# Seven-product gate/up stage: first-half token tiles turned and summed under the last two cross-attention outputs, second-half blocks loaded in place

## The chip, the cores and the metric

One core of one Trainium2 chip. The metric is the device time of one execution in microseconds (us): for the kernel before 2898.38, the median of 3 runs (2897.5 to 2900.68).

## What is computed

One decoder layer on x (2048 tokens of width D = 1024, float32): a token mixer, a cross-attention to 256 memory tokens, and a gated channel mixer of width 2816. The change touches the end of the second and the beginning of the third:

```python
...
    x = x + rmsnorm(xo @ w_xo, g_x_post)

    hf = rmsnorm(x, g_ffn_pre)
    ff = (jax.nn.silu(hf @ w_gate) * (hf @ w_up)) @ w_down
    x = x + rmsnorm(ff, g_ffn_post)
```

rmsnorm(x, g) is x * rsqrt(mean(x*x) + eps) * g, token by token.

## The kernel before, in words

TensorE's instructions stand in the order of the program. A scheduler orders the other engines' (VectorE, ScalarE, GpSimd, and SP, which issues the DMAs), and buffers come from pools that rotate. Tokens come in tiles of 128, so x is 16 tiles, 0 to 15. Precision: each float32 operand is split into a high part, a ScalarE cast to fp32r (L142), and a low part, a VectorE subtraction (L143); a product is hi·hi + hi·lo + lo·hi, three times the matmuls.

**Cross-attention outputs.** `c_out(t)` (L1091 on) makes the output of token tile t in 48 matmuls 128x512 (L1095), 24 for each half of the columns, then squares and sums it (ScalarE), scales it by gain and adds x (VectorE), takes the next norm's factor `rx2`, and stores the tile.

**Seven products.** gate and up use Strassen's scheme with seven products in place of eight. The tokens come in two halves of 8 tiles (first half tiles 0 to 7, second half 8 to 15). Even and odd token tiles on one side, the two halves of K = 1024 on the other, make 2 x 2 blocks; from these come seven operand blocks: B11 and B21 of the even tiles, B22 of the odd ones, and T1 = odd0 - even0, T2 = odd1 - T1, T3 = odd1 - odd0, T4 = T2 - even1, where 0 and 1 are the halves of K. Each block holds [128, 2 (hi, lo), 4, 512] numbers. The 22 column tiles of w_gate and of w_up come in 11 column pairs. `weights()` (L1246) loads a pair's weights (buffers `wr`), forms the weight sums on GpSimd (L1257 to L1263) and splits them into `w`, from a ring of ten buffers (`w4t`). `product` (L1273) makes 12 matmuls 128x512; a block takes 12 for gate and 12 for up, a pair 7 x 24 = 168. The order of the blocks in a pair is B11, T2, B21, T3, T1, T4, B22, into four PSUM tiles; sums of products on VectorE and the SwiGLU (L1280, L1281) follow, and `g` is stored.

**Tiles of the first half.** `d_load` (L1123) loads a tile `xtD` and multiplies it by `rx2` and the gain in one VectorE operation (L126); `d_transposed` turns it with 8 TensorE transposes (L1133) into PSUM. `d_even` (L1144) splits the turned tile into B11 and B21 and keeps a copy `hf`; `d_odd` (L1153) forms T1, T2, T3 (VectorE) and T4 (GpSimd, L1169) and splits them and B22. The loaded tiles rotate through the pool `tk` of three buffers, which also holds the last cross-attention tiles. The even tiles 0, 2, 4, 6 are turned under the outputs of tiles 14 and 15; the odd tiles 1, 3, 5, 7 inside the first pair, after its first products.

**Tiles of the second half** are turned one at a time between the first-half pairs 0 to 8 (`d_even_kept`, `d_odd_kept`, L1176 to L1199). Their blocks are kept as float32 in DRAM (`hc_d`); GpSimd makes the differences (L1192 to L1195). The even tile's copy `hf` has a pool of its own (`fh`); the odd tile's copy `ho` and its differences `t12` come from the ring of ten weight buffers.

**Half switch.** Behind the last pair of the first half the seven blocks are loaded back (L1354 to L1357), each in two halves of 512 KB through one buffer `hst`, and split again. The 11 pairs of the second half follow, and then the down product, whose weights `wd` are split by L142 and L143 as well (L1366 on).

Of the kernel before, what the change touches and what calls it, by code (L numbers as in the profile page):

```python
# [10 lines left out]
F32 = mybir.dt.float32  # L11
F32R = mybir.dt.float32r
# [37 lines left out]
def layer(ctx, tc, a, out):  # L50
# [1093 lines left out]
    def d_even(hc, t):  # L1144

        pt = d_transposed(t)
        for i, n in enumerate(("B11", "B21")):
            put(hc, n, t % 8 // 2, pt[:, i * 512:(i + 1) * 512])
        hf = ev.tile([P, T], F32, name="hf", tag="ev")
        sc.copy(hf, pt)  # L1150
        return hf

    def d_odd(hc, t, hf):  # L1153

        j = t % 8 // 2
# [12 lines left out]
        t4 = h12[:, 512:]
        gp.tensor_tensor(t4, t2, hf[:, 512:], ALU.subtract)  # L1169
        put(hc, "T4", j, t4)  # L1170
        put(hc, "B22", j, pt[:, 512:])

    def keep(name, j, src):
        sp.dma_start(hc_d[name][:, :, j * P:(j + 1) * P], q4(src))

    def d_even_kept(t):  # L1176
        pt = d_transposed(t)
        hf = fh.tile([P, T], F32, name="hf", tag="hf")
        sc.copy(hf, pt)
        for i, n in enumerate(("B11", "B21")):  # L1180
            keep(n, t % 8 // 2, hf[:, i * 512:(i + 1) * 512])
        return hf

    def d_odd_kept(t, hf):
        j = t % 8 // 2
        pt = d_transposed(t)
# [12 lines left out]
        keep("T3", j, hf[:, 0:512])  # L1199
# [9 lines left out]
    for t in range(NT):  # L1209
# [9 lines left out]
        if t == NT - 2:  # L1219
            esM.close()  # L1220
            esD = ExitStack()
            hpa = pool(esD, "hpa")
            ev = pool(esD, "ev", 4)
            gf = gain("g_ffn_pre")
            hc = {n: hpa.tile([P, 2, 4, 512], F32R, name="h" + n) for n in ("B11", "B21")}
            d_load(0)
            d_load(2)
            hfs = {}
# [56 lines left out]

    def pair(hv, n, hc, mids=()):
        mids = dict(mids)
        gens = [weights(w_, n) for w_ in (wg, wu)]
        pts, s = {}, {}

        def both(h, name, start, stop):
            if start:
                pts[name] = ps.tile([P, T], F32, name="pgu", tag="mm")
            for i in range(2):
                w = next(gens[i])
                product(pts[name], i, w, hc[h], start, stop)
                if (h, i) in mids:
                    mids[h, i]()
# [5 lines left out]
        both("B11", "X", True, False)
        s["1"] = ev.tile([P, T], F32, name="s1", tag="ev")
        sc.copy(s["1"], pts["X"])
        both("T2", "Y", True, False)
        s["16"] = ev.tile([P, T], F32, name="s16", tag="ev")
        v.tensor_tensor(s["16"], pts["Y"], s["1"], ALU.add)
        both("B21", "X", False, True)  # L1310
        sg = half.tile([P, 512], F32, name="sg", tag="half")
        swiglu(*lo_hi(pts["X"]), hv, 0, f, sg)
        both("T3", "Y", False, True)
        v.tensor_tensor(s["1"], pts["Y"], s["1"], ALU.add)
        both("T1", "Z", True, False)
# [3 lines left out]
        both("T4", "W", True, True)  # L1319
# [3 lines left out]
        both("B22", "Z", False, True)  # L1323
# [28 lines left out]
    for n in HC:  # L1352
        hc[n] = (hpa if n in ("B11", "B21") else hpb).tile([P, 2, 4, 512], F32R, name="h" + n)
# [117 lines left out]
```

## Time and profile before

| | |
|---|---|
| median of 3 runs | 2898.38 us (2897.5 to 2900.68) |
| the profiled execution's own time | 2900.78 us |
| its span on the core | 2899.0 us |
| mean granted TensorE clock | 0.981 of full speed |
| busy share of the span | TensorE 95%, VectorE 52%, ScalarE 38%, GpSimd 16% |
| DMA, mean over the span | 111 GB/s |

The span is what the profiler saw of the core from its first to its last instruction; the execution's own time is 1.78 us longer. Busy shares are means over stages with different limits, so a stage is read from its own waits and its own timeline. PE is TensorE, DVE VectorE, ACT ScalarE, POOL GpSimd, SP (in rows SPq) the engine that issues the DMAs; L1273 is line 1273 of the kernel. Names in rows have no buffer numbers: `pgu` is the PSUM tile of gate and up, `pt` a turned tile, `pxo` an output of the cross-attention, `hB` and `hT` the operand blocks, `w` a split weight.

### The profile page before, as it was taken

The page shows a single profiled execution, that of the slowest core. Times are in us where ns is not written, and L with a number is a line of the kernel's source. Part 1 is how long each engine was busy: PE and PEld are TensorE (multiplying, and loading weights), DVE is VectorE, ACT ScalarE, POOL GpSimd, SP SyncE. Part 2 cuts the span into 40 slices and gives each one's busy share as a digit, 9 for nine tenths or more (in the row PEclk, how much of TensorE's full clock was granted, in tenths as well). Part 3 has the DMA queues.
Part 4 walks back from the last instruction along what each step waited for, and adds up shares of the span by engine and source line. Part 5 has one row for each costly group of instructions (what it writes and reads, how often), then busy time and mean ns, then how long its engine had stood idle before and what let it go on. Part 6 is the DMA issues. An engine that isn't in the chain of part 4 may idle for free.

```text
span 2899.0 us, 35143 instructions
## 1 busy us (share of the span) xinstructions
PE 2767.6 (95%) x13420; PEld 2293.9 (79%) x13420; DVE 1510.5 (52%) x2393; ACT 1087.7 (38%) x2294; POOL 464.1 (16%) x337
## 2 busy tenths in 40 slices
PE   9989989999989999999979999997999999999998
PEld 6778768888877888888858777786888887888887
DVE  4363367787886555333475555555454543122244
ACT  4232137677776444222252333233333333120122
POOL 0000012212240000000013433331333210000022
PEclk9999989999999999999989999998999999999999
DMA  5443563534442543111133343334222234131153
GB/s 185 131 168 106 171 199 112 152 105 135 132 147 68 173 166 116 44 44 44 59 109 98 120 124 108 103 113 130 77 80 88 84 95 134 48 105 51 37 171 119
DMA packets 239713, 322.82 MB, mean 111 GB/s; under 512 B 14776, under 2 KB 183864, under 8 KB 239544
## 3 DMA queue, kind: packets, MB, share of 16 engines
q1 hardware_dynamic: 239224, 319.52, 34.7%
q8 instruction: 106, 1.74, 0.3%
q0 software_dynamic: 320, 1.05, 0.1%
q14 instruction: 63, 0.52, 0.1%
HBM read 224.96 MB, written 95.55 MB: 111 GB/s over the span
## 4 chain that ended last, share of the span: by engine, by line
PE 78%; DVE 8%; DMA 4%; ACT 3%; issue 1%; POOL 1%; SPq 0%; DVEq 0%; ACTq 0%; POOLq 0%
PE pgu L1273 26%; PE pdn L1385 16%; PE pxo L1095 6%; PE psc L1056 6%; PE pmix L870 5%; PE S L731 3%; PE o L792 3%; PE pu L287 2%; DVE p L773 2%; DVE nmx L738 2%; PE pv L303 2%; PE T L783 1%; PE pqk L287 1%; PE o L537 1%; PE S L870 1%
## 5 line engine op out<-in xcount | busy, mean ns | idle before, releaser
L1273 PE MATMUL pgu<-hT,w 128*128 128x512 f32 x2112 | 495.3, 394 | 27.6 <-ACT hT L142 21.0
L1273 PEld LDWEIGHTS pgu<-hT,w 128*128 128x128 f32 x2112 | 400.9, 190 | 115.8 <-ACT hT L142 22.3
L1385 PE MATMUL pdn<-wd,g 128*128 128x512 f32 x2112 | 481.7, 390 | 4.2 <-DVE wd L143 3.5
L1385 PEld LDWEIGHTS pdn<-wd,g 128*128 128x128 f32 x2112 | 397.3, 188 | 88.4 <-DVE wd L143 4.7
L1273 PE MATMUL pgu<-hB,w 128*128 128x512 f32 x1584 | 375.0, 394 | 16.5 <-ACT w L142 10.0
L143 DVE TENSOR_TENSOR w<-wr,w 128x512 fp32r<-128x512 f32 (+3 forms) x382 | 260.3, 707 | 214.7 <-ACT w L142 213.8
L1273 PEld LDWEIGHTS pgu<-hB,w 128*128 128x128 f32 x1584 | 299.5, 190 | 82.2 <-ACT w L142 11.2
L142 ACT CAST w<-wr 128x512 fp32r<-128x512 f32 (+3 forms) x384 | 202.0, 557 | 343.7 <-PE pgu L1273 206.4
L731 PE MATMUL S<-kt,q 128*128 128x512 f32 (+2 forms) x640 | 181.5, 399 | 34.6 <-ACT p L747 33.5
L747 ACT ACTIVATE p<-S,nmx 128x1024 f32<-128x1024 f32 (+3 forms) x192 | 167.4, 873 | 95.5 <-DVE nmx L740 44.1
L1257 POOL TENSOR_TENSOR s<-wr 128x512 f32<-128x512 f32 x44 | 62.3, 1416 | 878.1 <-PE pxo L1095 524.9
L738 DVE TENSOR_REDUCE nmx<-S 128x1 f32<-128x1024 f32 (+3 forms) x192 | 173.3, 908 | 47.5 <-PE S L734 37.2
L287 PE MATMUL pqk<-hT,w 128*128 128x512 f32 x768 | 180.9, 397 | 4.0 <-ACT w L142 4.0
L1095 PE MATMUL pxo<-VW,pT 128*128 128x512 f32 x768 | 183.3, 397 | 0.4 <-ACT pT L142 0.4
L1056 PE MATMUL psc<-Mq,h 128*128 128x512 f32 x768 | 178.9, 392 | 0.0
L287 PEld LDWEIGHTS pqk<-hT,w 128*128 128x128 f32 x768 | 145.6, 190 | 39.0 <-ACT w L142 4.9
L142 ACT CAST g<-gr 128x1024 fp32r<-128x1024 f32 (+1 forms) x48 | 47.1, 982 | 338.5 <-PE pdn L1385 301.4
L1095 PEld LDWEIGHTS pxo<-VW,pT 128*128 128x128 f32 x768 | 143.1, 188 | 33.3 <-ACT pT L142 0.6
L1056 PEld LDWEIGHTS psc<-Mq,h 128*128 128x128 f32 x768 | 143.0, 188 | 29.3
L731 PEld LDWEIGHTS S<-kt,q 128*128 128x128 f32 x640 | 111.5, 196 | 59.1 <-ACT p L747 44.1
L870 PE MATMUL pmix<-wo,in 128*128 128x512 f32 x624 | 145.2, 394 | 0.0
L870 PEld LDWEIGHTS pmix<-wo,in 128*128 128x128 f32 x624 | 117.1, 188 | 27.5
(294 smaller groups left out, 3580.6 us busy)
## 6 DMA issues: line engine op xcount, KB each, us to landing
wr<-in_w_gate SPq DMA_DIRECT2D x44, 512.0 KB
wr<-in_w_up SPq DMA_DIRECT2D x44, 512.0 KB
wr<-in_w_in SPq DMA_DIRECT2D x32, 512.0 KB
q<-qk_q SPq DMA_DIRECT2D x128, 128.0 KB
gr<-g SPq DMA_DIRECT2D x32, 512.0 KB
g<-s SPq DMA_DIRECT2D x44, 256.0 KB
wr<-in_w_down SPq DMA_DIRECT2D x22, 512.0 KB
xt<-in_x SPq DMA_DIRECT2D x16, 512.0 KB
```

Source lines behind the costliest of these rows:

```text
L142: sc.copy(dst_hi, src)
L143: (eng or v).tensor_tensor(dst_lo, src, dst_hi, ALU.subtract)
L287: pe.matmul(pt[:, ch * 512:(ch + 1) * 512], w[ws][:, k, :], hT[ch][hs][:, k, :], start=(n == 0), stop=(n == 23))
L731: pe.matmul(st[:, c0:c0 + cwm], x["qs"][s][:, m, q0:q0 + P], x["kst"][m][pc][:, c0:c0 + cwm], start=(s == 0), stop=(s == 1 and not last))
L738: v.tensor_reduce(nmx[:, pc:pc + 1], st[:, :w_], AX.X, ALU.max, negate=True)
L747: sc.activation(pt[:, :w_], st[:, :w_], AF.Exp, bias=nmx[:, pc:pc + 1], accum_out=x["l2"][:, m, pc:pc + 1])
L792: pe.matmul(ot[:, :P], aT[b // 4][:, (b % 4) * P:(b % 4 + 1) * P], vt[b // 8][:, b % 8, :], start=(b == 0), stop=(b == i))
L870: pe.matmul(pt[:, ch * 512:(ch + 1) * 512], iT[is_][:, k * P:(k + 1) * P], w[ws][:, ch * 512:(ch + 1) * 512], start=(n == 0), stop=(n == 23))
L1056: pe.matmul(pt[:, ch * 512:(ch + 1) * 512], h2[hs][:, k, :], Mq[k][ms_][:, ch * 512:(ch + 1) * 512], start=(n == 0), stop=(n == 23))
L1095: pe.matmul(pt[:, ch * 512:(ch + 1) * 512], pT[ps_][:, k, :], VW[k][vs][:, ch * 512:(ch + 1) * 512], start=(n == 0), stop=(n == 23))
L1273: pe.matmul(pt[:, i * 512:(i + 1) * 512], w[:, ws, k, :], h[:, hs, k, :], start=(start and n == 0), stop=(n == 11), skip_group_check=not s ...
L1385: pe.matmul(pt[:, ch * 512:(ch + 1) * 512], gs[gi][:, f, :], ws[f][:, wi, ch * 512:(ch + 1) * 512], start=(f == 0 and n == 0), stop=(f == ...
```

## The change

Four parts.

1. All eight tiles of the first half are turned under the outputs of tiles 14 and 15 (`two`): a pair of token tiles ahead of each output, and one between its two halves. The gain product of these tiles is a ScalarE scale and a GpSimd product (`d_load` with an engine) instead of one VectorE operation. B11, B21, T1 and T2 are written there. The differences T3 and T4 are both made on GpSimd and stay in float32 until the cross-attention's weights have left their memory; then T3, T4 and B22 are split. The first pair's instructions are released only behind the last odd tile's copy (`tc.issue_after`).
2. The order of the products is B11, T2, B21, T1, T3, T4, B22.
3. For kept tiles, `ho` and `t12` come from a pool `st4` of two buffers, and the even tile's copy `hfk` from the pool of the gains; so the gain `g_ffn_post` is loaded after the last kept store.
4. At the half switch each block (1 MB) is loaded by one DMA into its own low half; ScalarE casts from there into the high half, VectorE subtracts in place.

```diff
-    HC = ("B11", "T2", "B21", "T3", "T1", "T4", "B22")
+    HC = ("B11", "T2", "B21", "T1", "T3", "T4", "B22")
...
-    def d_load(t):
+    def d_load(t, eng=None):
         xt = tk.tile([P, D], F32, name="xtD", tag="tk")
         sp.dma_start(xt, x2_d[t])
-        norm(xt, gf, xt, rx2[:, t:t + 1])
+        if eng is None:
+            v.scalar_tensor_tensor(xt, xt, rx2[:, t:t + 1], gf, ALU.mult, ALU.mult)
+        else:
+            sc.activation(xt, xt, AF.Copy, scale=rx2[:, t:t + 1])
+            eng.tensor_tensor(xt, xt, gf, ALU.mult)
         dn[t] = xt
...
         h12 = w4t("h12", F32)
-        sc.copy(h12[:, 0:512], pt[:, 0:512])
+        last_h[0] = sc.copy(h12, pt).ins
...
         put(hc, "T2", j, t2)
-        t3 = h12[:, 0:512]
-        v.tensor_tensor(t3, pt[:, 512:], t3, ALU.subtract)
-        put(hc, "T3", j, t3)
         put(hc, "T1", j, t1)
-        t4 = h12[:, 512:]
-        gp.tensor_tensor(t4, t2, hf[:, 512:], ALU.subtract)
-        put(hc, "T4", j, t4)
-        put(hc, "B22", j, pt[:, 512:])
+        gp.tensor_tensor(hf[:, 512:], t2, hf[:, 512:], ALU.subtract)
+        gp.tensor_tensor(hf[:, 0:512], h12[:, 512:], h12[:, 0:512], ALU.subtract)
+        return hf, h12
...
-        hf = fh.tile([P, T], F32, name="hf", tag="hf")
+        hf = gpool.tile([P, T], F32, name="hfk", tag="gain")
...
-        ho = w4t("ho", F32)
+        ho = st4.tile([P, T], F32, name="ho", tag="st4")
...
-        t12 = w4t("t12", F32)
+        t12 = st4.tile([P, T], F32, name="t12", tag="st4")
...
         d0 = 4 * (t - NT + 2)
-        hfs[d0] = d_even(hc, d0)
-        c_out(t, *pr, mid=lambda: hfs.update({d0 + 2: d_even(hc, d0 + 2)}))
-        if d0 == 0:
-            d_load(4)
-            d_load(6)
+
+        def two(x, more=()):
+            rest8.append(d_odd(hc, x + 1, d_even(hc, x)))
+            for m in more:
+                d_load(m, gp)
+
+        two(d0, (3, 4) if d0 == 0 else (7,))
+        c_out(t, *pr, mid=lambda: two(d0 + 2, (5, 6) if d0 == 0 else ()))
     esV.close()
...
+    for j, (hf, h12) in enumerate(rest8):
+        put(hc, "T3", j, hf[:, 0:512])
+    for j, (hf, h12) in enumerate(rest8):
+        put(hc, "T4", j, hf[:, 512:])
...
+    for j, (hf, h12) in enumerate(rest8):
+        put(hc, "B22", j, h12[:, 512:])
+    ev = pool(esD, "ev", 4)
+    st4 = pool(esD, "st4", 2)
...
         if n == 0:
-            pair(0, 0, hc, [(("B11", 0), odd_pair(1, 5)), (("B11", 1), lambda: (odd_pair(3, 7)(), odd_pair(5, None)(), odd_pair(7, 8)()))])
+            with tc.issue_after(last_h[0]):
+                pair(0, 0, hc)
+            d_load(8)
             continue
...
+        hi, lo = hc[n][:, 0], hc[n][:, 1]
+        move(lo, hc_d[n])
         for i in range(2):
-            st = st4.tile([P, 2, 512], F32, name="hst", tag="st4")
-            sp.dma_start(st, hc_d[n][:, 2 * i:2 * i + 2, :])
-            split(hc[n][:, 0, 2 * i:2 * i + 2, :], hc[n][:, 1, 2 * i:2 * i + 2, :], st)
+            ks = slice(2 * i, 2 * i + 2)
+            sc.copy(hi[:, ks], lo[:, ks].bitcast(F32))
+            v.tensor_tensor(lo[:, ks], lo[:, ks].bitcast(F32), hi[:, ks], ALU.subtract)
...
-    gfp = gain("g_ffn_post")
+    with tc.issue_after(last_h[0]):
+        gfp = gain("g_ffn_post")
```

Where the instructions stand, at three places. In these rows the numbers behind names tell buffers apart.

VectorE of the changed kernel, from the end of the last output to the first weights of the second block, T2. `e_q` to `rx2` is the norm's factor of tile 15, `w_13755` is T2's gate weight and `w_13771` its up weight:

```order
L106 TENSOR_SCALAR ms_q_13651<-ssq_13649 128x1
L143 TENSOR_TENSOR hT4_13667<-hf_13588,hT4_13667 128x4x128
L143 TENSOR_TENSOR w_13755<-wr_13707,w_13755 128x512
L112 SCALAR_TENSOR_TENSOR e_q_13657<-r0_q_13655,ms_q_13651 128x1
L143 TENSOR_TENSOR hB22_13688<-h12_13359,hB22_13688 128x4x128
L113 TENSOR_SCALAR e_q_13657<-e_q_13657 128x1
L143 TENSOR_TENSOR hB22_13688<-h12_13427,hB22_13688 128x4x128
L115 TENSOR_TENSOR rx2_142<-r0_q_13655,e_q_13657 128x1
L143 TENSOR_TENSOR hB22_13688<-h12_13535,hB22_13688 128x4x128
L143 TENSOR_TENSOR hB22_13688<-h12_13599,hB22_13688 128x4x128
L143 TENSOR_TENSOR w_13771<-wr_13729,w_13771 128x512
```

The last splits of T4 and all of B22, which the first pair's last two blocks read, now stand ahead of the second block's up weight.

ScalarE around kept tile 9, the first odd one, before (`ho` is its copy, `s1` and `s16` belong to the pair ahead, `w_14253` to `w_14310` are the first weights of the pair behind):

```order
L1280 ACTIVATE s1_14012<-s1_14012 128x512
L1188 COPY ho_14230<-pt_14221 128x1024
L1280 ACTIVATE s16_14047<-s16_14047 128x512
L142 CAST w_14253<-wr_14246 128x512
L142 CAST w_14275<-wr_14268 128x512
L142 CAST w_14294<-wr_14246 128x512
L142 CAST w_14310<-wr_14268 128x512
```

and of the change, where `w_14375` to `w_14421` are weights of the pair behind:

```order
L142 CAST w_14375<-wr_14258 128x512
L1293 ACTIVATE c22_14159<-c22_14159 128x512
L142 CAST w_14391<-wr_14280 128x512
L1293 ACTIVATE s1_14024<-s1_14024 128x512
L142 CAST w_14406<-s3_14262 128x512
L142 CAST w_14421<-s3_14284 128x512
L1188 COPY ho_14242<-pt_14233 128x1024
L1293 ACTIVATE s16_14059<-s16_14059 128x512
```

The next pair's weight casts moved from behind the copy `ho` to ahead of it.

SP (the DMA issues) at the half switch, before:

```order
L1356 DMA hst_16653<-hc_B11_10719 128x1024
L508 DMA wr_16734<-in_w_up 128x4x256
L508 DMA wr_16736<-in_w_up 128x4x256
L1356 DMA hst_16658<-hc_T2_10720 128x1024
L1283 DMA g_002_10709<-sg_16506 128x4x128
L1356 DMA hst_16662<-hc_T2_10720 128x1024
L1356 DMA hst_16667<-hc_B21_10721 128x1024
```

and of the change:

```order
L101 DMA hB11_16660<-hc_B11_10719 128x2048
L508 DMA wr_16725<-in_w_up 128x4x256
L101 DMA hT2_16666<-hc_T2_10720 128x2048
L508 DMA wr_16727<-in_w_up 128x4x256
L101 DMA hB21_16672<-hc_B21_10721 128x2048
L1296 DMA g_002_10709<-sg_16518 128x4x128
L101 DMA hT1_16678<-hc_T1_10722 128x2048
L101 DMA hT3_16684<-hc_T3_10723 128x2048
```

A block's two loads became one, and the first two blocks' loads stand ahead of the two weight loads of `w_up`, one each.

## Rows read from the trace of the kernel before

**Rows 1.** The page, its first section: busy time, share of the span, instructions.

```profile
PE 2767.6 (95%) x13420; PEld 2293.9 (79%) x13420; DVE 1510.5 (52%) x2393; ACT 1087.7 (38%) x2294; POOL 464.1 (16%) x337
```

**Rows 2.** Waits of PE, 1500 to 2900 us: total us, times, longest.

```profile
PE pgu L1273 <- ACT hT L142: 21.0, 3, 10.4
```

**Rows 3.** Timeline of PE, start of the stage: start us, us, instruction, [idle before <-releaser].

```profile
1460.74 1.04 PE L1133 MATMUL pt<-cst,xtD 128*128 128x128 f32 x8
...
1488.05 2.90 PE L1273 MATMUL pgu<-hB,w 128*128 128x512 f32 x12
...
1526.24 5.60 PE L1273 MATMUL pgu<-hB,w 128*128 128x512 f32 x24
```

**Rows 4.** Timeline of PE around the half switch.

```profile
1967.76 5.60 PE L1273 MATMUL pgu<-hT,w 128*128 128x512 f32 x24
...
2029.94 5.60 PE L1273 MATMUL pgu<-hT,w 128*128 128x512 f32 x24
...
2068.02 5.60 PE L1273 MATMUL pgu<-hT,w 128*128 128x512 f32 x24
```

**Rows 5.** Timeline of PE, kept tiles 8, 9 and 10, and later.

```profile
1553.45 1.03 PE L1133 MATMUL pt<-cst,xtD 128*128 128x128 f32 x8
...
1592.45 1.03 PE L1133 MATMUL pt<-cst,xtD 128*128 128x128 f32 x8
...
1636.71 1.03 PE L1133 MATMUL pt<-cst,xtD 128*128 128x128 f32 x8
...
1891.60 5.60 PE L1273 MATMUL pgu<-hT,w 128*128 128x512 f32 x24
```

**Rows 6.** Timeline, one tile's load and its gain product.

```profile
1411.24 0.32 SPq L1125 DMA_DIRECT2D xtD<-x  x1
...
1414.69 1.28 DVE L126 SCALAR_TENSOR_TENSOR xtD<-xtD,rx,gain_g_ffn_pre 128x1024 f32<-128x1024 f32 x1 [0.22 <-DMA xtD<-x]
```

**Rows 7.** Groups by line and form: busy us, mean ns, idle before.

```profile
L1437 POOL TENSOR_TENSOR y<-y,wr 128x1024 f32<-128x1024 f32 x15 | 36.0, 2398 | 494.2 <-DVE y L1436 482.7 <-issue 5.8 <-DMA gr<-g 5.8
...
L1169 POOL TENSOR_TENSOR h<-t,hf 128x512 f32<-128x512 f32 x4 | 5.5, 1382 | 14.8 <-DVE t L1162 14.8
...
L1042 ACT ACTIVATE Mq<-wr,cs 128x1024 fp32r<-128x1024 f32 x5 | 5.7, 1149 | 3.6 <-DMA wr<-mq 3.6
```

**Rows 8.** Window of PE: stretch, us, busy (count), PEclk, DMA share, GB/s.

```profile
1596.00:1598.00 2.00, 2.00 (x6) 0.50 0.90 282
```

**Rows 9.** Timeline around kept tile 9, the first odd one.

```profile
1593.58 1.01 ACT L1188 COPY ho<-pt 128x1024 f32<-128x1024 f32 x1 [4.49 <-PE pt L1133]
...
1595.02 1.13 ACT L142 CAST w<-wr 128x512 fp32r<-128x512 f32 x2
...
1595.68 7.37 PE L1273 MATMUL pgu<-hB,w 128*128 128x512 f32 x24 [2.19 <-ACT w L142]
...
1601.03 1.20 SPq L1174 DMA_DIRECT2D hc_T<-hf  x2
```

**Rows 10.** Timeline in the last first-half pair: blocks loaded and split.

```profile
1944.48 3.51 POOL L1260 TENSOR_TENSOR wr<-wr 128x512 f32<-128x512 f32 x2
...
1946.77 1.77 DVE L143 TENSOR_TENSOR w<-wr,w 128x512 fp32r<-128x512 f32 x1
1946.88 0.33 SPq L1356 DMA_DIRECT2D hst<-hc_T  x1
...
1950.57 1.05 ACT L142 CAST hT<-hst 128x1024 fp32r<-128x1024 f32 x1 [1.92 <-DMA hst<-hc_T]
...
1951.65 1.23 DVE L143 TENSOR_TENSOR hT<-hst,hT 128x1024 fp32r<-128x1024 f32 x1 [1.37 <-ACT hT L142]
1952.79 0.68 DVE L143 TENSOR_TENSOR w<-wr,w 128x512 fp32r<-128x512 f32 x1
```

**Rows 11.** Timeline of ACT, end of the second half.

```profile
2403.78 1.98 ACT L142 CAST wd<-wr 128x1024 fp32r<-128x1024 f32 x2
...
2407.40 1.28 ACT L1363 ACT_TABLE_LOAD   x1
```

More of the change, by code (lines that the diff above doesn't have):

```diff
@@ L1148, in d_even @@
             put(hc, n, t % 8 // 2, pt[:, i * 512:(i + 1) * 512])
-        hf = ev.tile([P, T], F32, name="hf", tag="ev")
+        hf = (tk if t == 6 else hfp).tile([P, T], F32, name="hf", tag="tk" if t == 6 else "hf")
         sc.copy(hf, pt)
@@ L1222, in layer @@
             hpa = pool(esD, "hpa")
-            ev = pool(esD, "ev", 4)
+            esH = ExitStack()
+            hfp = pool(esH, "hfp", 3)
             gf = gain("g_ffn_pre")
[L1225 to L1228, printed above, removed]
+            hc = {n: hpa.tile([P, 2, 4, 512], F32R, name="h" + n) for n in HC[:4]}
+            rest8, last_h = [], [None]
+            for i in range(3):
+                d_load(i, gp)
         d0 = 4 * (t - NT + 2)
-        hfs[d0] = d_even(hc, d0)
-        c_out(t, *pr, mid=lambda: hfs.update({d0 + 2: d_even(hc, d0 + 2)}))
-        if d0 == 0:
-            d_load(4)
-            d_load(6)
-    esV.close()
-    hpb = pool(esD, "hpb")
-    st4 = pool(esD, "st4", 1)
-    fh = pool(esD, "fh", 1)
+        def two(x, more=()):
[4 more added lines that the diff above has]
+        c_out(t, *pr, mid=lambda: two(d0 + 2, (5, 6) if d0 == 0 else ()))
+    esV.close()
+    hpr = right(esD, "hpr")
+    hcp = {n: hpa for n in HC[:4]} | {"T3": hpr, "T4": hpr}
+    for n in ("T3", "T4"):
+        hc[n] = hpr.tile([P, 2, 4, 512], F32R, name="h" + n)
+    for j, (hf, h12) in enumerate(rest8):
+        put(hc, "T3", j, hf[:, 0:512])
+    for j, (hf, h12) in enumerate(rest8):
+        put(hc, "T4", j, hf[:, 512:])
+    esH.close()
+    hcp["B22"] = pool(esD, "hpb")
+    hc["B22"] = hcp["B22"].tile([P, 2, 4, 512], F32R, name="hB22")
+    for j, (hf, h12) in enumerate(rest8):
+        put(hc, "B22", j, h12[:, 512:])
+    ev = pool(esD, "ev", 4)
+    st4 = pool(esD, "st4", 2)
     half = pool(esD, "half", 3)
-    for n in HC:
-        if n not in hc:
-            hc[n] = hpb.tile([P, 2, 4, 512], F32R, name="h" + n)
     def weights(wsrc, n):
@@ L1263, in weights, with product @@
         gp.tensor_tensor(a12, a12, a11, ALU.subtract)
+        yield out(a21)
         yield out(s3)
-        yield out(a21)
         yield out(a22)
         yield out(a12)
-    def product(pt, i, w, h, start, stop):
+    def product(pt, i, w, h, start):
         n = 0
@@ L1284, in swiglu, with pair, both @@
                      dst.rearrange("p (t c) -> p t c", t=4))
-    def pair(hv, n, hc, mids=()):
-        mids = dict(mids)
+    def pair(hv, n, hc):
         gens = [weights(w_, n) for w_ in (wg, wu)]
         pts, s = {}, {}
-        def both(h, name, start, stop):
+        def both(h, name, start):
             if start:
@@ L1294, in both @@
             for i in range(2):
[L1295 to L1298, printed above, removed]
+                product(pts[name], i, next(gens[i]), hc[h], start)
         def lo_hi(x):
@@ L1303, in pair @@
         f = 2 * n
[L1304 removed]
+        both("B11", "X", True)
         s["1"] = ev.tile([P, T], F32, name="s1", tag="ev")
         sc.copy(s["1"], pts["X"])
[L1307 removed]
+        both("T2", "Y", True)
         s["16"] = ev.tile([P, T], F32, name="s16", tag="ev")
         v.tensor_tensor(s["16"], pts["Y"], s["1"], ALU.add)
[L1310 removed]
+        both("B21", "X", False)
         sg = half.tile([P, 512], F32, name="sg", tag="half")
         swiglu(*lo_hi(pts["X"]), hv, 0, f, sg)
[L1313 removed]
+        both("T1", "Z", True)
+        both("T3", "Y", False)
         v.tensor_tensor(s["1"], pts["Y"], s["1"], ALU.add)
[L1315 removed]
         c22 = ev.tile([P, T], F32, name="c22", tag="ev")
@@ L1322, in pair @@
         swiglu(*lo_hi(c21), hv, 0, f + 1, c21[:, 0:512])
-        both("B22", "Z", False, True)
+        both("B22", "Z", False)
         c12 = s["16"]
@@ L1352, in layer @@
     for n in HC:
-        hc[n] = (hpa if n in ("B11", "B21") else hpb).tile([P, 2, 4, 512], F32R, name="h" + n)
+        hc[n] = hcp[n].tile([P, 2, 4, 512], F32R, name="h" + n)
+        hi, lo = hc[n][:, 0], hc[n][:, 1]
+        move(lo, hc_d[n])
         for i in range(2):
-            st = st4.tile([P, 2, 512], F32, name="hst", tag="st4")
-            sp.dma_start(st, hc_d[n][:, 2 * i:2 * i + 2, :])
-            split(hc[n][:, 0, 2 * i:2 * i + 2, :], hc[n][:, 1, 2 * i:2 * i + 2, :], st)
+            ks = slice(2 * i, 2 * i + 2)
+            sc.copy(hi[:, ks], lo[:, ks].bitcast(F32))
+            v.tensor_tensor(lo[:, ks], lo[:, ks].bitcast(F32), hi[:, ks], ALU.subtract)
     for n in range(NPAIR):
```

12 lines of the change are left out of this document (2 added, 10 removed).

## The prediction

> **What bounds the kernel now.** I read the page first: TensorE is busy in 95% of the span [rows 1], so only its gaps can be won. Then TensorE's own list of waits from the seven-product stage on: the largest is for ScalarE's casts of the operand blocks [rows 2]. TensorE's order in time then shows three places with gaps, and the change touches each. (a) Start: the first gate/up product begins at 1488.05, and the block T2 (second of seven) is finished only at 1526.24 [rows 3], though two blocks are 48 matmuls. A whole pair is 168 matmuls and repeats every 2068.02 - 2029.94 = 38.08 us [rows 4], 0.227 us each, so 48 of them are 10.9 us: 27.3 us of the 38.2 are turning and waiting. (b) Kept tiles: the step from one turning to the next is 39.0 us with an even tile and 44.3 us with an odd one [rows 5]. (c) Half switch: the first pair of the second half takes 2029.94 - 1967.76 = 62.2 us from its T2 to the next T2, against 38.08 [rows 4].
>
> **(a) The start.** Taken out behind 1488.05: four turnings, their splits and TensorE's waits. Added ahead of it: the same four turnings, under the outputs of token tiles 14 and 15. VectorE's gain product of eight tiles becomes a ScalarE scale and a GpSimd product; T4's difference stays on GpSimd and T3's joins it. Before, the stretch from the first turning (1460.74) to 1488.05 is 27.3 us; four more turnings of at most 1.04 us [rows 3] make it 31.5 us if TensorE never waits.
>
> It will wait. Token tile 15 sits in one of the three tk buffers, so the feed-forward tiles rotate through two: tile n+2 is loaded when tile n is turned. Its chain is the load, 3.45 us from issue to use [rows 6], the scale, by the nearest row 1.15 us, and the GpSimd product, by the nearest row 2.40 us [rows 7]: 7.0 us. Between the products of two tiles GpSimd makes a 512-wide difference of 1.38 us [rows 7], so the second tile of a token pair is ready 7.0 + 1.38 + 2.40 = 10.8 us after the pair ahead frees its first buffer. TensorE comes there after 24 matmuls and two turnings, 7.2 us (5.44 and some 1.8). Each of the three later pairs is 3.6 us late: 10.8 us. After such gaps the granted clock falls: behind one odd tile's gap it stood at 0.50, the 1.2 GHz level [rows 8]; there 24 matmuls took 7.37 us where others take 5.60 [rows 3, 9], so one such spell costs 1.8 us. The outputs then end at 1460.7 + 31.5 + 10.8 + 1.8 = 1504.8, 16.8 us later than now.
>
> What is queued there next is on VectorE: the splits of T3, T4 and B22 stand ahead of the up weights of T2. From the end of the outputs VectorE has, all from SBUF, 15 splits of 0.68 us and one wide operation of 1.23 us, 11.4 us, and GpSimd seven differences of 1.38 us, 9.7 us. These two do not overlap: two GpSimd subtractions take 3.51 us, and VectorE's split behind them, 0.68 us when alone, takes 1.77 us and ends 0.55 us after GpSimd is done [rows 10]. So they add up: 21.1 us, and the last quarter of T2's matmuls 0.9: T2 is done at 1526.8, where it is 1526.2 now. **I put the first part at nothing**: it moves work, and the work stays late. Bounds: if the split queue overlaps GpSimd, 9.7 us sooner; if ScalarE's square of tile 15, ahead of which weight casts wait for GpSimd and behind which VectorE's T2 splits wait, comes late, some 6 us later.
> The Trainium skill (SBUF — State Buffer, section Who interferes with whom) says that a VectorE instruction with two SBUF inputs and a GpSimd instruction that reads SBUF keep each other out, the second until the first ends. The rows agree; had the two been independent, as the split of work between engines supposes, the forecast would be 2847 us.
>
> **(b) Kept tiles.** Now the odd tile's copy `ho` takes its buffer from the ring of ten that also holds the weight blocks. ScalarE therefore casts the pair's first weights only behind it: `ho` at 1593.58, the weights at 1595.02, TensorE idle 2.19 us and slow after [rows 9]. The change gives `ho` and `t12` two buffers of their own, and the order puts the next pair's weight casts ahead of `ho`, and GpSimd's weight sums ahead of the tile's four differences: exactly as with an even tile, which costs nothing [rows 5]. From 1553.45 to 1891.60 stand eight pairs and one block: 338.15 - 5.44 - 8 x 39.0 = **20.7 us to win**. Below, 14 us if one in three odd tiles still waits. GpSimd's differences now come behind the sums; they have the rest of the 38 us pair, and only the stores read them.
>
> **(c) Half switch.** Now each half block goes through one buffer: issue at 1946.88, cast at 1950.57, subtraction 1951.65 to 1952.88 [rows 10], 6.1 us with the next issue; 14 of these are some 85 us, for blocks that TensorE uses every 5.44 us. The change loads a whole block (1 MB) into its own low half when that block's last product is done: no shared buffer. Block k is free 5.4(k+1) us into the last pair of the first half and needed 38.1 + 5.4k us into it, 32.6 us later. It needs the load, the trace's 512 KB take 3.7 us, so at most 7.4 us for twice that, two casts of 1.05 us and two subtractions of 1.23 us: 12 us. Thus 20 us are spare. On SP the moves stand ahead of two weight loads; these go out when the first two blocks are free, near where they go now, so nothing behind them is late. Of the 62.2 - 38.1 = 24.1 us I take **22.3 us**, and leave one slow-clock spell of 1.8 us for VectorE, which carries all 14 subtractions in some 43 us beside its usual work. Bounds 16 and 24.
>
> **Down stage.** Now two w_down casts run at 2403.78, ahead of the last SwiGLU and the table load, which ends at 2408.7 [rows 11]. In the new order all stand behind them, for their memory is in use to the last product. The first cast moves back some 5 us, but four more weights wait for buffers anyway: **1.5 us lost**, bounds 0 and 4.
>
> **Sum.** 0 + 20.7 + 22.3 - 1.5 = 41.5 us. The profiled execution took 2900.8 us (span 2899.0), 2.4 us over the median of 2898.4; taken from that median: **2857 us**. The best ends together give 2857 - 9.7 - 1.7 - 1.5 = 2844, the worst ones 2857 + 6 + 6.7 + 6.3 + 2.5 = 2879. (From here 0.2%, 5.8 us, is what a measurement can tell from no change.)
>
> **Rivals.**
> 1. The turning hides altogether: GpSimd and the loads keep pace with TensorE, the outputs end 4.2 us later and T2 10.9 us after that, at 1503. Then 24 us more are won: 2833. For it: VectorE is rid of eight gain products. Against: two buffers and the 7.0 us chain. 0.10.
> 2. At the half switch VectorE becomes the bound: 17 us of subtractions, its usual work and GpSimd's turns fill the pair, and half the gap stays: 2857 + 11.2 = 2868. For it: VectorE waits behind GpSimd [rows 10]. Against: weights are split up to ten products ahead. 0.10.
> 3. The eight gain products hold VectorE: each, 2.40 us long, keeps out the SBUF splits of T1 and T2 and with them the probabilities of tile 15; the pairs come another 19 us late, T2 ends near 1546: 2876. The Trainium skill's rule above (same page and section) is this mechanism, for an operation twice as wide as any beside VectorE here. 0.14.
> 4. **Slower**: only one buffer is left for the kept even tile's copy (the other holds the gain). The copy stands in ScalarE's queue ahead of weight casts and must wait until the odd tile's last differences are stored. Now those stores issue at 1601.03 [rows 9], 8.6 us after that tile's turning and 35.7 us before the next even one [rows 5]. Each us beyond that is lost at three tiles; it turns the gain into a loss once GpSimd is later by 35.7 + 41.5/3 = 50 us; 20 us beyond give 2917. GpSimd has some 8 sums of 1.4 us and 4 differences in a pair, so against. 0.06.
> 5. The weight casts do not get ahead of `ho`, since the first ones wait for buffers released late: (b) gives nothing, 2878. 0.04.
>
> **How the numbers follow.** The forecast's case has 0.56, from 2844 to 2872; the rivals 0.44. The range 2833 to 2880 goes from rival 1's own time to the worst ends; it leaves out rival 4, the half of rival 1 below its time and a few per cent where rivals 2, 3 and 5 meet. Faster 0.90; within 0.2% 0.04, where rivals 3 and 5 come together; slower 0.06.
>
> **What would show it.** Right: TensorE's gaps between the outputs' halves of 2 to 4 us, the first product 12 to 18 us later than now with T2's second half waiting for VectorE's weight split; odd steps of 39.0 us; no gap over 2 us at the half switch; no `hst`. Wrong: T2 finished before 1515 or after 1540, odd steps near 44, or waits for hT casts in the second half.

## The result, and the profile after

The changed kernel takes 2861.8 us (median of 4 runs, 2859.6 to 2862.0), the kernel before 2897.9 (4 runs): a ratio of 0.9875, 95% interval 0.9858 to 0.9892. The forecast was 2857 us, range 2833 to 2880. The gain is 36 us by the medians; the two profiled executions, 2900.8 and 2861.6 us, are 39.2 apart.

First the page of the changed kernel, busy times as in [rows 1]:

```profile
PE 2764.2 (97%) x13420; PEld 2289.0 (80%) x13420; DVE 1493.3 (52%) x2381; ACT 1099.7 (38%) x2302; POOL 485.6 (17%) x349
```

TensorE does the same work in a shorter span; what went are gaps. Its waits from 1500 us on (total, times, longest), which answer to [rows 2]:

```profile
PE pgu L1286 <- ACT w L142: 5.4, 1, 5.4
PE pdn L1389 <- ACT wd L142: 4.3, 1, 4.3
PE pgu L1286 <- DVE w L143: 3.9, 1, 3.9
PE pgu L1286 <- DVE c L1326: 0.7, 2, 0.5
PE pdn L1389 <- DVE wd L143: 0.5, 1, 0.5
```

No wait for casts of operand blocks is left. To see where each microsecond went, I cut both traces at the same events of TensorE: the first turned tile, the first product, the end of T2, tile 8's turning, T2 of the first half's last pair but one, T2 of the second half's second pair, the first down product. The windows of the kernel before (stretch, us, busy time and instructions of PE, PEld, DVE, ACT and POOL, granted clock, DMA share, GB/s):

```profile
1440.00:1460.74 20.74, 20.74 (x95) 16.95 (x95) 7.58 (x18) 5.04 (x12) 0.00 (x0) 1.00 0.17 60
1460.74:1488.05 27.31, 26.95 (x137) 22.36 (x136) 17.53 (x30) 14.33 (x30) 0.00 (x0) 1.00 0.33 102
1488.05:1526.24 38.19, 19.31 (x81) 14.61 (x80) 36.47 (x55) 22.83 (x44) 15.50 (x11) 0.78 0.34 110
1526.24:1553.45 27.21, 27.21 (x122) 22.48 (x121) 22.01 (x23) 9.69 (x15) 16.01 (x10) 1.00 0.35 107
1553.45:1891.60 338.15, 323.75 (x1434) 265.34 (x1432) 184.08 (x193) 100.16 (x163) 118.17 (x81) 0.99 0.37 114
1891.60:2029.94 138.34, 122.66 (x506) 99.48 (x504) 79.07 (x83) 48.98 (x71) 36.39 (x24) 0.93 0.38 119
2029.94:2405.30 375.36, 375.36 (x1658) 310.81 (x1656) 185.95 (x221) 119.36 (x185) 103.79 (x71) 1.00 0.29 86
```

and of the changed kernel (its last stretch ends inside the wait ahead of the down product):

```profile
1440.00:1458.40 18.40, 18.40 (x86) 15.13 (x85) 7.38 (x16) 4.41 (x10) 0.28 (x1) 1.00 0.15 49
1458.40:1499.00 40.60, 34.32 (x169) 28.08 (x168) 30.19 (x39) 28.21 (x48) 24.18 (x13) 0.92 0.37 121
1499.00:1523.43 24.43, 15.13 (x49) 11.38 (x48) 23.11 (x32) 16.33 (x34) 15.48 (x10) 0.72 0.17 65
1523.43:1551.44 28.01, 27.82 (x121) 22.39 (x120) 24.75 (x26) 9.55 (x15) 14.88 (x10) 1.00 0.39 116
1551.44:1871.38 319.94, 319.94 (x1433) 263.48 (x1432) 172.96 (x193) 104.30 (x163) 114.85 (x81) 1.00 0.41 120
1871.38:1987.36 115.98, 115.50 (x506) 94.54 (x505) 77.22 (x83) 48.56 (x71) 37.75 (x24) 1.00 0.46 146
1987.36:2370.00 382.64, 378.78 (x1657) 310.66 (x1655) 185.93 (x224) 119.36 (x186) 98.68 (x71) 1.00 0.29 85
```

Row by row the changed kernel stands, in us: 2.3 sooner ahead of anything that was changed, so this is not the change's (in the experiments that leave that part alone the first turned tile stands between 1454.1 and 1461.3); 13.3 longer to the first product; 13.8 shorter from there to the end of T2; 0.8 longer; **18.2 shorter** over the kept tiles; **22.4 shorter** over the half switch; 3.4 longer over the second half, counted to the end of its last product, which lies 4.3 us of wait before the first down product at 2370.48. The down stage, with that wait and to each span's end, is equal within 0.2.

Two rows were not expected: the second half, which the change does not touch, is 3.4 us longer, and the kept stretch won less than it should while TensorE never pauses there (319.94 of 319.94 us). The timeline of TensorE in a pair of the changed kernel's second half shows why (start us, us, instruction):

```profile
1987.36 5.60 PE L1286 MATMUL pgu<-hT,w 128*128 128x512 f32 x24
1992.80 5.60 PE L1286 MATMUL pgu<-hB,w 128*128 128x512 f32 x24
1998.23 16.79 PE L1286 MATMUL pgu<-hT,w 128*128 128x512 f32 x72
2014.87 11.06 PE L1286 MATMUL pgu<-hB,w 128*128 128x512 f32 x48
2025.76 5.60 PE L1286 MATMUL pgu<-hT,w 128*128 128x512 f32 x24
```

The pair takes 2025.76 - 1987.36 = 38.40 us, against 38.08 [rows 4]. T2 and B21 still take 5.44 us each; the three blocks T1, T3, T4 take 2014.87 - 1998.23 = 16.64 where three times 5.44 is 16.32. The starts of single matmuls put it all on T3 and T4: they follow each other by 0.233 us, those of the other five blocks by 0.227. There is no idle time and the clock is at its upper level, so no list of waits can show it. In the compiled program T3 and T4 are the only blocks at the right end of the memory: they begin at bytes 196576 and 212960 of a partition, 2016 above a multiple of 2048; the other blocks and the weights `w` begin 1888 above one.

### The profile page after: what moved, and what is told of

The parts are those of the page before. It is cut to its first block, busy times and chain, and to the rows that moved or that the text cites. A ratio compares the mean times of both kernels' runs of the same rounds, so it can differ in the third digit from the quotient of the medians.

```text
span 2859.7 us, 35163 instructions
## 1 busy us (share of the span) xinstructions
PE 2764.2 (97%) x13420; PEld 2289.0 (80%) x13420; DVE 1493.3 (52%) x2381; ACT 1099.7 (38%) x2302; POOL 485.6 (17%) x349
## 4 chain that ended last, share of the span: by engine, by line
PE 80%; DVE 8%; DMA 3%; ACT 3%; issue 1%; POOL 1%; SPq 0%; DVEq 0%; ACTq 0%; POOLq 0%
PE pgu L1286 28%; PE pdn L1389 17%; PE psc L1056 6%; PE pxo L1095 5%; PE pmix L870 5%; PE S L731 3%; PE o L792 3%; PE pqk L287 2%; PE pu L287 2%; DVE p L773 2%; DVE nmx L738 2%; PE pv L303 2%; PE T L783 1%; PE S L870 1%; PE o L537 1%
## 5 line engine op out<-in xcount | busy, mean ns | idle before, releaser
L1286 PE MATMUL pgu<-hB,w 128*128 128x512 f32 x1584 | 369.1, 390 | 0.7 <-DVE c L1326 0.7
L792 PE MATMUL o<-vt,aT 128*128 128x128 f32 x1088 | 136.9, 281 | 0.0
```

Source lines behind the costliest of these rows:

```text
L792: pe.matmul(ot[:, :P], aT[b // 4][:, (b % 4) * P:(b % 4 + 1) * P], vt[b // 8][:, b % 8, :], start=(b == 0), stop=(b == i))
L1286: pe.matmul(pt[:, i * 512:(i + 1) * 512], w[:, ws, k, :], h[:, hs, k, :], start=(start and n == 0), stop=(n == 11), skip_group_check=not s ...
```

## The experiments

Times are medians of 4 or 5 runs; ratios, with their 95% intervals, are to the kernel before, run beside them.

**1. T3 and T4 moved by 128 bytes.**

```diff
+    right(esD, "pad").tile([P, 32], F32, name="pad")
     hpr = right(esD, "hpr")
```

> The changed kernel with T3 and T4 placed 128 bytes lower in SBUF, nothing else. In the changed kernel a matmul that reads T3 or T4 starts 0.233 us after the one ahead, one that reads another block 0.227 us, and a pair takes 38.41 us where it took 38.08. Theory (place in memory): the two blocks begin 32 bytes below a multiple of 2048, all others 160 bytes below one; moved to the others' offset they run at 0.227, the pair takes 38.08 us and 21 or 22 pairs give back 0.33 us each: 7 us, about 2855 us. Rival (the order of the products, or the region of memory above the other blocks): the step stays at 0.233 and the time within 1 us of the changed kernel's 2861.8.

Measured 2853.3 us, ratio 0.9853 (0.9839 to 0.9866). TensorE's timeline of this kernel:

```profile
2028.71 16.48 PE L1287 MATMUL pgu<-hT,w 128*128 128x512 f32 x72
2045.03 11.04 PE L1287 MATMUL pgu<-hB,w 128*128 128x512 f32 x48
```

T1, T3 and T4 take 16.32 us again. The place in memory costs 0.32 us in each of 22 pairs, 7.0 us. The medians are 8.5 us apart and the intervals of the two ratios overlap, so the 7.0 us rest on the rows.

**2. The whole right end moved by 128 bytes.** The same pad as the first allocation of the kernel.

> The changed kernel with everything that it allocates from the right end of SBUF placed 128 bytes lower. Theory (place in memory): not T3 and T4 alone, but also the cross-attention weights VW, the output projection's wo and the first weights begin 32 bytes below a multiple of 2048; their matmuls start 0.229 to 0.238 us apart. With 768 of the outputs and 432 of the output projection at 0.227 too, some 4.6 and 2.6 us come on top of the 7 us of T3 and T4, and a few more from the first projections: 2843 to 2850 us. Rival (only T3 and T4 are slow, for a reason of their own): as the kernel with these two moved alone, about 2855 us, or no gain at all.

Measured 2843.4 us, ratio 0.9813 (0.98 to 0.9827): 10 us more than in experiment 1. So matmuls elsewhere were slow too, the outputs' and the first projections': by the starts of single matmuls both step at 0.233 us in the changed kernel and at 0.227 here. But the first projections' moving operand already lay at 1888, and their weights at 2016: a bad place of the moving operand alone can't be the rule. Experiment 8 takes this up.

**3. The kept odd tile back in the weight ring.**

```diff
-        ho = st4.tile([P, T], F32, name="ho", tag="st4")
+        ho = w4t("ho", F32)
...
-        t12 = st4.tile([P, T], F32, name="t12", tag="st4")
+        t12 = w4t("t12", F32)
```

> The changed kernel with the odd kept tile's copy and differences taken from the ring of weight buffers again. Theory (buffers): the next pair's first weights wait for the copy again; the four odd steps go from 39.3 back to 44 or 45 us and the time to 2880 to 2884 us. Rival (the order that came with the other edits is what helps, the ring is not short): odd steps stay at 39.3 us and the time within 3 us of 2861.8.

Measured 2883.7 us, ratio 0.9955 (0.9938 to 0.9972), 22 us above the changed kernel. TensorE's timeline, tiles 8 to 10 and the wait behind tile 9:

```profile
1554.47 1.03 PE L1137 MATMUL pt<-cst,xtD 128*128 128x128 f32 x8
1593.78 1.04 PE L1137 MATMUL pt<-cst,xtD 128*128 128x128 f32 x8
1597.01 2.11 PE L1286 MATMUL pgu<-hB,w 128*128 128x512 f32 x8 [2.19 <-ACT w L142]
...
1605.28 7.40 PE L1286 MATMUL pgu<-hT,w 128*128 128x512 f32 x24 [1.78 <-ACT w L142]
1640.04 1.03 PE L1137 MATMUL pt<-cst,xtD 128*128 128x128 f32 x8
```

The even step is 39.3 us, the odd one 46.3, with the same 2.19 us ahead of the first weights as in [rows 9]. The buffers are the cause, with the order of the queues that follows from them.

**4. The blocks of the second half staged again, through two buffers.**

```diff
-        move(lo, hc_d[n])
         for i in range(2):
             ks = slice(2 * i, 2 * i + 2)
-            sc.copy(hi[:, ks], lo[:, ks].bitcast(F32))
-            v.tensor_tensor(lo[:, ks], lo[:, ks].bitcast(F32), hi[:, ks], ALU.subtract)
+            st = st4.tile([P, 2, 512], F32, name="hst", tag="st4")
+            sp.dma_start(st, hc_d[n][:, ks, :])
+            split(hi[:, ks], lo[:, ks], st)
```

> The changed kernel with the second half's blocks loaded in halves through a staging pool and split from there, as before, but with the pool's two buffers in place of one. Theory (the single buffer's round of 6.1 us, fourteen times, was the whole gap): with two buffers a block passes every 6.1 us against the 5.4 us in which TensorE uses one, with 32 us of lead; no gap over 2 us, at most 3 us slower than 2861.8. Rival (loading in place is what helps, since the staged splits stand in the queues of ScalarE and VectorE among the weights'): the gap of 12 to 24 us comes back, 2874 to 2886 us.

Measured 2864.2 us, ratio 0.9891 (0.9878 to 0.9905). What is left at the switch, in TensorE's timeline:

```profile
1873.09 5.60 PE L1286 MATMUL pgu<-hT,w 128*128 128x512 f32 x24
...
1941.18 11.15 PE L1286 MATMUL pgu<-hB,w 128*128 128x512 f32 x48 [2.00 <-DVE c L1326]
...
1958.38 5.73 PE L1286 MATMUL pgu<-hB,w 128*128 128x512 f32 x24 [0.60 <-ACT s L1315]
...
1991.47 5.60 PE L1286 MATMUL pgu<-hT,w 128*128 128x512 f32 x24
```

Loading in place is not needed to win the 22 us: with a second staging buffer the stretch of the half switch, T2 to T2, is 1991.47 - 1873.09 = 118.4 us, where it was 138.3 before and is 116.0 in place, so 20 of the 22.4 us come. In place these two waits of 2.6 us are one of 0.48; by the runs the two can hardly be told apart, their intervals overlap.

**5. The gain product on VectorE.** `if eng is None:` becomes `if True:` in `d_load`.

> The changed kernel with the gain product of the first eight tiles as one VectorE operation again, in place of a ScalarE scale and a GpSimd product. Theory (the chain of a tile, 7.0 us through GpSimd, is what TensorE waits for between the outputs' halves, and GpSimd's eight products, 19 us, delay its differences and weight sums): the chain becomes 4.7 us, TensorE's four waits for GpSimd's product, 5.6 us in all, go, and its wait of 5.4 us for T2's first weight shrinks; 4 to 8 us faster, 2854 to 2858 us. Rival (VectorE sets the end of the start): its eight operations of 1.28 us, 10 us, stand among the splits and the softmax of tile 15, T2 is done 3 to 8 us later, 2865 to 2870 us.

Measured 2857.5 us, ratio 0.9865 (0.9851 to 0.9878): by the medians 4.4 us faster than the changed kernel, though the intervals overlap. The trace is clearer. The first turned tile stands at the same time as in the changed kernel (1458.39 and 1458.40), the first product at 1494.10 where it was 1499.00, and T2 ends at 1517.34 where it was 1523.43. The waits of TensorE for the tiles go from 5.6 to 0.5 us, while the one for T2's first weight grows from 5.4 to 7.3 and one for the probabilities `pT` of tile 15 from 0.65 to 2.7. So the chain through GpSimd cost some 5 us.

**6. B22's splits behind T2.** The loop that splits B22 is called from the first pair, behind its second block.

> The changed kernel with the splits of B22 written behind the first pair's block T2, so that on VectorE T2's up weight stands ahead of them. Theory (the queue on VectorE, as predicted): TensorE's wait of 3.9 us between T2's halves shrinks by the four splits of 0.68 us, 2.7 us; 2859 us. Rival (the wait is for the norm's chain of tile 15, which stands there too, or for GpSimd): no change beyond 1 us, 2861 to 2863 us.

Measured 2861.9 us, ratio 0.9882 (0.9868 to 0.9895): no change, and TensorE still waits 3.87 us between T2's parts. The rows of the changed kernel tell what holds it there:

```profile
1497.88 0.69 DVE L1165 TENSOR_TENSOR t<-pt,hf 128x512 f32<-128x512 f32 x1 [1.14 <-ACT hf L1154]
...
1507.57 1.78 POOL L1273 TENSOR_TENSOR wr<-wr 128x512 f32<-128x512 f32 x1
...
1509.38 0.62 ACT L142 CAST w<-wr 128x512 fp32r<-128x512 f32 x1 [1.36 <-POOL wr L1273]
...
1514.49 1.88 DVE L143 TENSOR_TENSOR hT<-hf,hT 128x512 fp32r<-128x512 f32 x3
1516.30 0.14 DVE L106 TENSOR_SCALAR ms_q<-ssq 128x1 f32<-128x1 f32 x1
...
1516.96 0.68 DVE L143 TENSOR_TENSOR w<-wr,w 128x512 fp32r<-128x512 f32 x1
```

GpSimd's sum lets ScalarE cast T2's gate weight, and TensorE makes the eight matmuls that read its high part. The other 16 wait for its low part, which stands in VectorE's queue; VectorE is busy there without a pause from 1497.88 on. Ahead of that low part are, among others, the splits of T3 and T4 (6.3 us), the norm and the scaling of tile 15 (5.3 us) and tile 8's gain product (2.25 us). So it is the gate weight, not the up weight, and B22's splits come only behind it. What each of the others is worth alone was not tried.

**7. The kernel before with its right end moved.** The pad of experiment 2 in the old kernel.

> The kernel before, with everything that it allocates from the right end of SBUF placed 128 bytes lower. Its seven blocks do not lie there, so a pair stays at 38.08 us. Theory (place in memory acts by itself, wherever an operand begins 32 bytes below a multiple of 2048): what the same shift gave the changed kernel beyond T3 and T4, 2853.3 - 2843.4 = 10 us, comes here too: 2885 us; and the change without its two misplaced blocks is worth 41 to 42 us, the 41.5 of the forecast. Rival (the gain of the shift belongs to the new layout): no change, 2895 us.

Measured 2886.4 us, ratio 0.9965 (0.9951 to 0.9978): the old kernel has these slow matmuls as well. Against it the changed kernel with the same shift, 2843.4, is 43 us faster: with T3 and T4 placed alike, the change is worth about what was forecast. The two profiled executions turn their first tile at 1446.3 and 1446.4 us, so they can be compared without the noise of what stands ahead: the spans are 2883.1 and 2842.3 us, 40.8 apart, where 41.5 was forecast.

**8. The left end moved instead.** The pad is the first allocation of the left end of the changed kernel, so that blocks and weights all lie at 2016, with T3 and T4.

> The changed kernel with everything that it allocates from the left end of SBUF placed 128 bytes higher, and the right end left as it is: now all operands begin 32 bytes below a multiple of 2048, the blocks, T3 and T4 among them, and the weights. Theory A (a place of its own is slow): all seven blocks and the down product's weights step at 0.233 us as T3 and T4 do, which adds 5 x 24 x 22 + 2112 matmuls at 0.0066 us, 31 us: 2890 us or more. Theory B (slow is a matmul whose moving operand and weights begin at different places, in the first projections too, where the blocks lay at the fast place and the weights at the slow one): all step at 0.227, T3 and T4 too, and the time is that of the kernel with the right end shifted, 2843 us.

Measured 2845.1 us, ratio 0.982 (0.9805 to 0.9836), and T3 and T4 are fast at the very place where they were slow:

```profile
2022.66 16.48 PE L1287 MATMUL pgu<-hT,w 128*128 128x512 f32 x72
2038.98 11.04 PE L1287 MATMUL pgu<-hB,w 128*128 128x512 f32 x48
```

Theory B: it is the place of the moving operand against that of the weights.

**9. Other distances** (one run with a profile). T4 is put 32 bytes below its place, T3 64 bytes.

> The changed kernel with T4 placed 32 bytes lower (64 bytes below a multiple of 2048) and T3 64 bytes lower (96 below one). If what is slow is a beginning within 32 bytes of the multiple, both step at 0.227 us. If it needs 128 bytes, both stay at 0.233. If a beginning at a multiple of 64 is better than any now, T4's step falls below 0.227.

2857.7 us. By the starts of single matmuls T4 steps at 0.234 us on average, T3 at 0.230. From the weights they lie 96 and 64 bytes apart (modulo 2048), where 128 gave 0.233 and nothing 0.227. All three answers written down were wrong, since they spoke of a place of its own; for distance they read: 64 bytes cost half, 96 and 128 all. T4 begins at a multiple of 64 there and gains nothing by it.

**10. A weight sum formed later.**

```diff
-        s3 = half.tile([P, 4, P], F32, name="s3", tag="half")
-        gp.tensor_tensor(s3, a11, a21, ALU.subtract)
         gp.tensor_tensor(a21, a21, a22, ALU.add)
...
+        s3 = half.tile([P, 4, P], F32, name="s3", tag="half")
+        gp.tensor_tensor(s3, a22, a11, ALU.subtract)
```

> The changed kernel with the weight difference s3 formed later, from a22 and the new a11 (the same value up to rounding), so that GpSimd's sums for T2 need no memory of the cross-attention's weights and can go in the 4.5 us in which GpSimd waits ahead of the first product. Theory (TensorE's 5.4 us ahead of T2 are GpSimd's queue: two differences of token tiles and two s3 ahead of T2's sums): that wait shrinks to 2 us or less, and with it the 3.9 us behind it, since the square of tile 15 stands behind the same casts; 4 to 7 us faster, 2855 to 2858 us. Rival (VectorE's splits and the norm of tile 15 hold T2 anyway): the wait moves to T2's second part; within 1 us of 2861.8.

Measured 2862.2 us, ratio 0.988 (0.9863 to 0.9896): a miss. TensorE's two waits are 4.46 and 4.26 us where they were 5.43 and 3.86. GpSimd's sum is done at 1501.5, but T2's weight is cast only at 1507.39, in ScalarE's queue behind the casts of T3 and T4: the next of several queues.

**11. All together, with the first weights ahead.** Experiments 2, 5 and 10, and the weights of the first pair's first three blocks written ahead of the splits of T3, T4 and B22:

```diff
+    with tc.issue_after(last_h[0]):
+        gens0 = [weights(w_, 0) for w_ in (wg, wu)]
+        first = [[next(g) for g in gens0] for _ in range(3)]
     hpr = right(esD, "hpr")
```

> The changed kernel with four edits together: the right end shifted by 128 bytes (as measured: 18 us), the gain product on VectorE (4 us), s3 later, and the first three blocks' weights of the first pair written ahead of the splits of T3, T4 and B22. If what T2 waits for at the start is the queues' order, its waits of 7.3 and 2.4 us (with the gain on VectorE) shrink to 2 us in all: 2832 to 2836 us. If tile 15's norm or the splits of T1 and T2 hold it, they stay: 2839 us.

Measured 2836.3 us, ratio 0.9786 (0.9767 to 0.9804), the fastest kernel here. TensorE's timeline at its start:

```profile
1483.93 5.75 PE L1291 MATMUL pgu<-hB,w 128*128 128x512 f32 x24 [0.24 <-ACT w L144]
...
1492.06 4.87 PE L1291 MATMUL pgu<-hT,w 128*128 128x512 f32 x20 [1.47 <-DVE hT L145]
1497.76 5.78 PE L1291 MATMUL pgu<-hB,w 128*128 128x512 f32 x24 [0.84 <-ACT s L1320]
...
1508.97 17.58 PE L1291 MATMUL pgu<-hT,w 128*128 128x512 f32 x64 [3.61 <-DVE w L145]
```

T2 ends 13.8 us behind the first product, 24.4 in the changed kernel. Part of it moves on: T1's weight, behind the splits of T3, T4 and B22, now costs 3.6 us. It is the queues' order that made the start late. Experiments 2 and 5 added up give an estimate of 2839 us, so little of the shorter start is left in the time, 3 us, which the intervals don't tell from nothing. The sum alone (experiment 10) gave nothing; whether the weights alone would have done it was not tried.

**12. The two later parts alone.** The kernel before with `ho`, `t12` and `hfk` in the new buffers and the blocks loaded in place; the first half is turned as before, and all seven blocks lie at 1888.

> The kernel before with the kept tiles' buffers and the loading in place alone: the first half's tiles are turned as before, the order of the products and the place of the blocks are the old ones (T3 and T4 at the others' offset). Theory (the first part is worth nothing, and its place for T3 and T4 costs 7 us): the gain is 18.2 + 22.4 of the two later parts and the 2.6 us that T3 and T4 took back from the eight kept pairs, 43 us, 2855 us, as the changed kernel with T3 and T4 moved has (2853.3). Rival (the first part earns what its earlier end of T2 shows, 2 to 3 us, or more by the shorter queue behind): 2858 us or more.

Measured 2851.9 us, ratio 0.9846 (0.9832 to 0.986), by the medians 10 us faster than the whole change, by the profiled spans 8.9. Its first turned tile, its first product, its end of T2 and its tile 8:

```profile
1458.73 1.03 PE L1133 MATMUL pt<-cst,xtD 128*128 128x128 f32 x8
...
1486.07 2.90 PE L1274 MATMUL pgu<-hB,w 128*128 128x512 f32 x12
...
1524.32 5.60 PE L1274 MATMUL pgu<-hB,w 128*128 128x512 f32 x24
...
1551.53 1.03 PE L1133 MATMUL pt<-cst,xtD 128*128 128x128 f32 x8
```

Against the first turned tile its outputs end 13.3 us sooner than in the changed kernel and its T2 0.6 us later. Tile 8 comes 1551.53 - 1458.73 = 92.8 us behind the first turned tile; in experiment 1, which has the whole change with T3 and T4 placed as here, it is 92.9. The first part moves the work and earns nothing; its place for T3 and T4 costs 7.0 us. What is left of the 8.9 us are short waits of the changed kernel at the half switch and ahead of the down product.

## Why the prediction was right, and where it was off

**(a) The start: right in its sum, in part by luck.** The outputs were to end 16.8 us later and T2 0.6 later; against the first turned tile they end 13.3 later and T2 0.5 sooner. "It moves work, and the work stays late" is what experiment 12 shows. But from the outputs' end to the end of T2 were to pass 22.0 us, and 24.4 did: 3.5 us too many ahead of that end and 2.4 too few behind it nearly cancel. Two steps were off. The waits for tiles were put at 10.8 us; they are 5.6, in four pieces, with slower matmuls behind them:

```profile
1467.18 1.09 PE L1137 MATMUL pt<-cst,xtD 128*128 128x128 f32 x8 [1.28 <-POOL xtD L1130]
1471.16 1.97 PE L1137 MATMUL pt<-cst,xtD 128*128 128x128 f32 x8 [2.88 <-POOL xtD L1130]
...
1482.28 1.09 PE L1137 MATMUL pt<-cst,xtD 128*128 128x128 f32 x8 [1.30 <-POOL xtD L1130]
1484.02 7.41 PE L1095 MATMUL pxo<-VW,pT 128*128 128x512 f32 x24 [0.65 <-DVE pT L143]
```

And B22's splits, counted into what holds T2, hold nothing (experiment 6). T3's and T4's splits do stand in VectorE's queue ahead of T2's weight, as forecast, but with them the norm and the scaling of tile 15, 5.3 us, which were there only as a bound of 6 us and one wide operation, and tile 8's gain product, 2.25 us, which was missing. GpSimd's term was too small as well: 9.7 us for seven differences, where its eight operations there take 14.1 us, 1498.65 to 1512.79.

That GpSimd and VectorE keep each other out holds in these rows: tile 8's gain product, 1.28 us when alone [rows 6], took 2.25, from 1502.56 to 1504.81, while GpSimd's difference ran from 1501.98 to 1503.72:

```profile
1501.98 1.74 POOL L1169 TENSOR_TENSOR hf<-t,hf 128x512 f32<-128x512 f32 x1
...
1502.56 2.25 DVE L1127 SCALAR_TENSOR_TENSOR xtD<-xtD,rx,gain_g_ffn_pre 128x1024 f32<-128x1024 f32 x1
```

It ended 1.09 us behind GpSimd, nearly its own time. The Trainium skill (SBUF — State Buffer, section Who interferes with whom) speaks of an exclusive lock between the two; these rows agree. Rival 3, which made 19 us of it, fell all the same: T2 ends at 1523.43, not near 1546, and with the products back on VectorE 6.1 us sooner, not 19 (experiment 5).

**(b) The kept tiles: the mechanism right, 2.5 us too much.** All steps are now alike, odd as even, and experiment 3 ties this to the buffers. 18.2 us came, not 20.7. The failing step is the 39.0 us of an even tile, taken as fixed: it is 39.3 now, by T3 and T4, and eight pairs take 2.6 back. In experiment 12, where they lie as before, all steps are 39.0 us.

**(c) The half switch: right.** 22.3 us forecast, 22.4 measured. That it comes so near is luck: the spell of slow clock set aside, 1.8 us, did not come, and T3 and T4 took 1.0 us in three pairs and short waits most of the rest. That the round through the single buffer was the bound is shown by [rows 10] and experiment 4 together: the same loads and splits with two buffers win 20 us.

**Down stage: 1.5 us forecast, nothing lost.** The first `wd` comes later, with a wait of 4.3 us in one piece; the kernel before lost 4.1 us in four short ones, by its list of waits from 1500 us on:

```profile
PE pdn L1385 <- DVE wd L143: 3.5, 3, 2.2
...
PE pdn L1385 <- ACT wd L142: 0.6, 1, 0.6
```

So the wait that the forecast added took the place of others that it left standing. The first `wd` cast did move behind the table load, as the order had it.

**What was missing** is a term: the change moves T3 and T4 to the other end of the memory, and that slows 48 matmuls of each pair, 7.0 us in 22 pairs. Without it the forecast of 2857 would have been 2 to 4 us too slow (experiment 1: 2853.3, and by its ratio 2855). The other rivals fell too. The turning does not hide altogether (rival 1: T2 at 1503). VectorE did not become the bound at the half switch (rival 2: half the gap stays); TensorE waits 0.48 us there. `hfk` waits for no store of a kept tile (rival 4): ScalarE's waits ahead of it are 0.8 us in all. And the weight casts did get ahead of `ho` (rival 5): all odd steps are 39.3 us.

## What to carry to other kernels

A gain comes from the place where TensorE waits last: the two shortages of buffers that held weights and blocks up were worth 40 us, the large rearrangement ahead of them nothing, since the work that it moved still stood in the queues ahead of T2's weights. When a stage that was not touched gets longer without a single wait, compare the starts of single matmuls, and then where their operands lie. Before loading in place, try a second staging buffer.

## What was not expected of the hardware

In the gate/up, down and cross-attention matmuls, a 128x512 float32r matmul follows the one ahead by 0.227 us when its moving operand and its weights begin at the same place modulo 2048 bytes, be that 1888 or 2016 (experiments 1 and 8), and by 0.230 at 64 bytes' distance, 0.234 at 96 (both from the one run of experiment 9) and 0.233 at 128 (the changed kernel). It acts on the kernel before too: 128 bytes of padding at the right end gave 10 us there and 18 in the changed kernel. Down products, whose operands lie alike, are at 0.227 in the kernel before as in these. Two groups do not fit so plainly. In the mixer's output projection 156 matmuls whose operands lie alike stand among three times as many whose operands don't, and step at 0.230; with the right end moved, when all lie alike, they step at 0.227. The mixer's score matmuls, `S` from `kt` and `q`, lie alike in every kernel and step at a median of 0.235 to 0.236 with or without the shift; what holds them was not tried. Which modulus counts, and why the distance does it, was not tried.
